# A decoder trunk on one core: a plain first pair for the output projection, and matmuls on constants at the start

## The chip, the cores and the metric

The kernel runs on one core of a Trainium2 chip. Time is device microseconds (us) of one execution. A core has a matrix engine (PE, with its weight loads shown apart as PEld), a vector engine (DVE), a scalar engine (ACT), GpSimd (POOL) and SyncE (SP). Each takes its instructions in the order in which they were written for it. In this kernel SP issues the loads of weights and POOL issues nearly all other transfers. PSUM is the memory that matmuls accumulate in; it is used here in banks.

## The reference

One step of a decoder trunk with two layers, on 520 tokens together (512 of a prompt, 8 of a sample group), width 2048, float32. Per layer:

```
z = rmsnorm(x) @ W_in                      # 2048 -> 8192: conv parts B, C, xc, g and retention parts q, k, v, g
y_conv = B * conv3(C * xc) * silu(g_conv)  # causal, three taps
y_ret  = groupnorm(retention(rope(q), rope(k), v)) * silu(g_ret)    # 4 heads
x = x + concat(y_conv, y_ret) @ W_out      # the output projection
x = x + sigmoid(x @ W_pg) * (p @ W_ple)    # the gate
```

After the second layer comes a last rmsnorm. The states of the convolution and of the retention are outputs too.

## The kernel before

Activations lie transposed: 128 features on the partitions, 520 tokens along a row, in two halves (LEFT and RIGHT) of 260. A projection from 2048 to 2048 has 16 tiles along K (what is summed over) and 16 along M (outputs). M tiles are made two at a time, as **pairs**. A float32 product is three matmuls in a reduced format: each operand is split into a high and a low part by ACT (high) and DVE (low), and high-high, high-low and low-high are added up in PSUM (lines 243, 244, 245). Weights are split in `split_w` (lines 225 and 226) into a ring of 60 tiles whose parts come free when PE has used them; raw weights lie in a ring of 32. Operands are split in `split` (lines 539 and 540).

A pair can be made with Strassen's scheme on its first `s` K tiles and plainly on the rest (`strassen`). It has two M tiles, two halves of the tokens and two halves of these K tiles, so 7 products in place of 8. In matmuls: a plain pair is 16 x 2 x 2 x 3 = 192; Strassen on s tiles takes 3s/2 off. For that DVE adds weights (line 308), and needs sums of operands (`operand_sums`, lines 410 to 413, two new tiles to split for each two K tiles). Partial results are copied from bank to bank and to SBUF while the pair runs, by `copy` (ACT) and `plus` (DVE), which all carry line 296.

How many K tiles each pair takes in Strassen is written in tables: `HEADS`, `CONVS`, `OUT_ROWS` and `GATES`, one list for each layer. `OUT_ROWS` is the output projection's. The class `Operands` builds the operands and their sums for a stage: its list `todo` says for which two K tiles the plain operand, the sums, or both are made, and in which order. Where a table has 0, `pair` makes two single M tiles by `gemm`, one after the other; the first `v` pair of layer 0 is such a one.

There are five PSUM banks for these accumulations (`acc`), handed out in the order in which they came free, and three more for smaller things. `Val` passes a pair's result on, either as SBUF tiles or as the banks themselves.

The order on each engine is not the order of the source. A scheduler places each engine's instructions by a model of time, with a higher priority for weight splits and for `copy` and `plus`. Between engines semaphores keep the dependences, and within an engine the order is fixed: an instruction that waits holds up all behind it.

At the start of the program the first three M tiles are made while inputs arrive, K tile by K tile (lines 655 to 690): SP loads weights and inputs, ACT and DVE split both. Layer by layer there follow the heads' pairs, the convolution's pairs (the last of them with s = 14), the output projection, and the gates.

## Time and profile before

| | |
|---|---|
| time, median of 3 runs | 2204.39 us (2201.32 to 2206.91) |
| the profiled execution: its own time | 2211.48 us |
| its span, first to last instruction | 2209.7 us |
| mean granted PE clock | 0.994 |
| PE busy | 98% of the span, 17854 matmul records |
| DVE, ACT, POOL busy | 86%, 58%, 20% |

The profile's busy shares are averages over stages. "Idle before, releaser" in its rows is the time that an engine stood still ahead of an instruction and the instruction that ended it. PEclk is the clock that PE was granted, 1.00 being all of it. Tile names are without buffer numbers: `ps_g` is any of the five banks, `slot` any of 75 SBUF tiles of 520 columns, `split` and `raw` the rings of weights.

### The profile page before, as it was taken

What the parts mean: (1) busy time and instruction counts of PE and PEld (TensorE: products, weight loads), DVE (VectorE), ACT (ScalarE), POOL (GpSimd) and SP (SyncE); (2) the same over time, 40 slices, a digit from 0 to 9 for tenths busy, and PEclk for the clock granted to TensorE, in tenths of its full rate; (3) what the DMA queues carried; (4) which work ended last, traced back from release to release, by engine and by line L of the source; (5) the groups of instructions that cost most, each with busy time, mean ns of one, the idle gap of its engine ahead of it and who ended that gap; (6) DMA issues with size and microseconds to landing.
All of it is one profiled execution on the core that took longest, in us unless ns stands there. A gap on an engine that the chain in (4) does not pass through costs nothing. (4 is left out here: it accounts for less than half of the span.)

```text
span 2209.7 us, 48509 instructions
## 1 busy us (share of the span) xinstructions
PE 2164.1 (98%) x17854; PEld 2153.7 (97%) x17854; DVE 1906.0 (86%) x3928; ACT 1291.3 (58%) x2789; POOL 443.1 (20%) x764
## 2 busy tenths in 40 slices
PE   8999999999999999999999999999999999999998
PEld 8999999999999899999989999999999999999997
DVE  7789998898999887787997998989998998888874
ACT  8555656555556554565775565655645565555655
POOL 3213222211002210211211222222110031121011
PEclk9999999999999999999999999999999999999999
DMA  7655565555443753745645566664555365556455
GB/s 255 192 170 195 179 222 175 187 160 163 148 144 124 246 172 115 245 150 178 204 143 186 164 205 195 190 214 154 158 172 159 115 197 173 170 187 212 132 161 187
DMA packets 189071, 392.10 MB, mean 177 GB/s; under 512 B 26720, under 2 KB 69728, under 8 KB 188832
## 3 DMA queue, kind: packets, MB, share of 16 engines
q1 hardware_dynamic: 134336, 214.38, 31.2%
q0 software_dynamic: 54496, 174.62, 23.8%
q8 instruction: 140, 2.29, 0.4%
q14 instruction: 99, 0.81, 0.1%
HBM read 323.74 MB, written 65.15 MB: 176 GB/s over the span
## 5 line engine op out<-in xcount | busy, mean ns | idle before, releaser
L243 PE MATMUL ps_g<-slot,split 128*128 128x260 f32 x5496 | 1549.8, 285 | 33.0 <-ACT ps_g L296 13.6
L244 PE MATMUL ps_g<-slot,split 128*128 128x260 f32 x5496 | 1550.8, 284 | 0.0
L245 PE MATMUL ps_g<-slot,split 128*128 128x260 f32 x5496 | 1535.8, 284 | 0.4 <-DVE split L226 0.4
L225 ACT ACTIVATE split<-raw 128x512 fp32r<-128x512 f32 (+2 forms) x1401 | 785.1, 580 | 624.6 <-DVE raw L308 206.7
L243 PEld LDWEIGHTS ps_g<-slot,split 128*128 128x128 f32 x5496 | 1035.6, 189 | 40.5 <-ACT ps_g L296 15.2
L244 PEld LDWEIGHTS ps_g<-slot,split 128*128 128x128 f32 x5496 | 1040.7, 189 | 0.3 <-DVE slot L543 0.3
L245 PEld LDWEIGHTS ps_g<-slot,split 128*128 128x128 f32 x5496 | 1032.6, 189 | 0.9 <-DVE split L226 0.9
L226 DVE TENSOR_TENSOR split<-raw,split 128x512 fp32r<-128x512 f32 (+2 forms) x1401 | 848.1, 627 | 185.4 <-ACT split L225 116.6
L308 DVE TENSOR_TENSOR raw<-raw 128x512 f32<-128x512 f32 (+2 forms) x688 | 427.0, 633 | 24.9 <-DMA raw<-wi 17.8
L296 ACT ACTIVATE slot<-ps_g 128x260 f32<-128x260 f32 x368 | 139.0, 380 | 123.4 <-PE ps_g L245 105.9
L540 DVE TENSOR_TENSOR slot<-slot,slot 128x520 fp32r<-128x520 f32 (+1 forms) x202 | 118.6, 616 | 4.6 <-ACT slot L539 4.0
L539 ACT ACTIVATE slot<-slot 128x520 fp32r<-128x520 f32 (+1 forms) x202 | 104.8, 570 | 11.4 <-DMA slot<-x1s 3.1
L764 POOL DMA_DIRECT2D o_rets<-slot x64 | 35.4, 553 | 344.2 <-DVE slot L763 132.9
L296 DVE TENSOR_TENSOR slot<-ps_g,slot 128x260 f32<-128x260 f32 x184 | 77.3, 421 | 7.6 <-PE ps_g L245 4.6
L1041 POOL DMA_DIRECT2D slot<-x1s x82 | 44.0, 538 | 159.3 <-DVE slot L540 56.2
L852 POOL DMA_DIRECT2D slot<-hs x64 | 46.2, 723 | 119.4 <-PE ps_st L245 31.3
L296 ACT ACTIVATE ps_g<-ps_g 128x260 f32<-128x260 f32 x146 | 54.4, 373 | 20.7 <-PE ps_g L245 20.3
L763 DVE SCALAR_TENSOR_TENSOR slot<-slot,vs,slot 128x256 f32<-128x256 f32 x128 | 55.9, 477 | 8.6 <-ACT slot L759 8.5
L797 POOL DMA_DIRECT2D hs<-slot x64 | 35.6, 557 | 134.5 <-DVE slot L738 66.4
L722 DVE TENSOR_TENSOR slot<-slot,slot 128x520 f32<-128x520 f32 x80 | 55.3, 691 | 7.6 <-DMA o_rets<-slot 7.0
L753 POOL DMA_DIRECT2D slot<-sret x64 | 35.3, 552 | 130.2 <-ACT split L225 36.3
L754 POOL DMA_DIRECT2D slot<-kq x64 | 34.8, 545 | 113.3 <-DVE slot L1090 18.5
(213 smaller groups left out, 1668.5 us busy)
## 6 DMA issues: line engine op xcount, KB each, us to landing
raw<-wi SPq DMA_DIRECT2D x377, 256.0 KB, 4.1
raw<-wi SPq DMA_DIRECT2D x136, 192.0 KB, 4.1
raw<-wo SPq DMA_DIRECT2D x96, 256.0 KB, 4.4
raw<-wg SPq DMA_DIRECT2D x88, 256.0 KB, 4.9
slot<-x1s POOLq DMA_DIRECT2D x82, 260.0 KB, 5.7
hs<-slot POOLq DMA_DIRECT2D x64, 256.0 KB, 3.9
slot<-sret POOLq DMA_DIRECT2D x64, 256.0 KB, 3.9
slot<-hs POOLq DMA_DIRECT2D x64, 256.0 KB, 4.8
```

The costliest lines, as they stand in the source:

```text
L225: S.activation(hi, raw, AF.Copy)
L226: V.tensor_tensor(lo, raw, F(hi), SUB)
L243: PE.matmul(out, wh, xh, start=start, stop=False, skip_group_check=more)
L244: PE.matmul(out, wh, xl, start=False, stop=False, skip_group_check=more)
L245: PE.matmul(out, wl, xh, start=False, stop=stop, skip_group_check=more)
L296: fn(*args)
L308: V.tensor_tensor(out[:, n], x[:, n], y[:, n], op)
L539: keep(S.activation(hi, src[:, n], AF.Copy))
L540: V.tensor_tensor(lo, src[:, n], F(hi), SUB)
L722: V.tensor_tensor(out[:, n], v, table[:, n], MUL)
L763: keep(V.scalar_tensor_tensor(st[:, c], k, vs[:, h, e, b : b + 1], st[:, c], MUL, ADD))
L852: SIDE.dma_start(t[:, :512].rearrange("p (m n) -> p m n", m=2), src)
```

## The change

Four things change; the tables' other lists stay.

1. `OUT_ROWS` goes from [4, 8, 12, 16, 16, 16, 16, 10] to [0, 8, 16, 16, 16, 16, 16, 10] for both layers. Both lists sum to 98, so the output projection has the same number of matmuls.
2. A new function `plain` serves pairs with 0: for each four K tiles it makes both M tiles, into four banks, and returns the banks themselves. It also takes the place of the two `gemm` calls for the first `v` pair of layer 0. `FIRST` keeps the order in which the output projection's operands are made (the first four K tiles with their sums at once), as it was.
3. Eight matmuls of `ones` on `onesd` (128x128, float32, result unused) stand ahead of PE's first work, and the load of `vec` is issued by ACT and not by SP.
4. In the gates the sigmoid is one instruction over 520 columns of an SBUF result, where it was two of 260.

```diff
--- before.py
+++ after.py
@@ -50,7 +50,7 @@
 
 HEADS = [[0, 0, 0, 4, 8, 12] + [14] * 10, [4, 8, 12] + [14] * 13]
 CONVS = [[14] * 2 + [16] * 13 + [14]] * 2
-OUT_ROWS = [[4, 8, 12, 16, 16, 16, 16, 10]] * 2
+OUT_ROWS = [[0, 8, 16, 16, 16, 16, 16, 10]] * 2
 
 MIXED, MIX = 64, [*range(8, 14), *range(8), 14, 15]
 OUTS = [[MIXED + s for s in r] for r in OUT_ROWS]
@@ -58,6 +58,8 @@
 WPRIO = 20
 LATE = 0
 RAW = 32
+WARM = 8
+FIRST = 4
 SPLIT = 60
 
 
@@ -275,6 +277,24 @@
                     product(ps[h], w, j - a, at(x.ops, ks[j : j + 1], n), j == 0, j == KT - 1)
             split_ring.put(*w)
         return Val(banks.put, ps=ps)
+
+    def plain(x, src0, src1):
+
+        ps = acc(4)
+        for a, b in chunks(0, KT):
+            x.supply(min(b + CH, KT))
+            for i, src in enumerate((src0, src1)):
+                w = parts(src, a, b)
+                for j in range(a, b):
+                    for h, n in enumerate((LEFT, RIGHT)):
+                        product(ps[2 * i + h], w, j - a, at(x.ops, [j], n), j == 0, j == KT - 1)
+                split_ring.put(*w)
+            if b == KT // 2:
+                while middle:
+                    middle.pop(0)()
+                aside()
+        aside()
+        return Val(banks.put, ps=ps[:2]), Val(banks.put, ps=ps[2:])
 
     def strassen(x, src0, src1, s, step=None):
 
@@ -390,13 +410,7 @@
         if s:
             z = strassen(x, src[m], src[m + 1], s, (lambda i: x.free(i, nxt)) if last else None)
         else:
-            z0 = gemm(x, src[m], s)
-            while middle:
-                middle.pop(0)()
-            aside()
-            z1 = gemm(x, src[m + 1], s)
-            aside()
-            z = z0, z1
+            z = plain(x, src[m], src[m + 1])
             if last:
                 x.free(8, nxt)
         x.release(n + 1)
@@ -426,7 +440,7 @@
             self.ops = [None] * KT
             self.sums = []
             self.ready = 0
-            first = rows[0] // 2
+            first = max(rows[0], min(FIRST, max(rows))) // 2
             self.todo = [(True, True)] * first + [(True, False)] * (KT // 2 - first)
             self.todo = [(i, *t) for i, t in enumerate(self.todo)]
             self.todo += [(i, False, True) for i in range(first, max(rows) // 2)]
@@ -640,6 +654,11 @@
             return rb
 
 
+    warm = pr.tile([P, 512], F32, tag="r", name="warm")
+    for i in range(WARM):
+        PE.matmul(warm[:, :P], ones, onesd, start=True, stop=True)
+
+
     over = pr.tile([P, 512], F32, tag="r", name="ps_r")[:, :TH]
     first = [acc(2), acc(2), acc(1) + [over]]
     def from_dram(src):
@@ -660,7 +679,7 @@
         if b == 1:
             raw = raw_ring.get(3)
             DMA.dma_start(raw.rearrange("p (m n) -> p m n", n=P), wi[0, 0:3, :, :P].rearrange("m p n -> p m n"))
-            DMA.dma_start(vec, vecs)
+            S.dma_start(vec, vecs)
             x = get()
             for n in (LEFT, RIGHT):
                 DMA.dma_start(x[:, n], xT[0, :, n])
@@ -1167,14 +1186,17 @@
             Gt.need(m // 2 + 1)
             for i, z in enumerate(zs):
                 x = xs[i]
-                for h, (n, ps) in enumerate(zip((LEFT, RIGHT), pes[2 * i : 2 * i + 2])):
-                    v = z.slot[:, n] if z.ps is None else z.ps[h]
-                    S.activation(v, v, AF.Sigmoid)
-                    V.tensor_tensor(v, v, ps, MUL)
-                    V.tensor_tensor(x[:, n], x[:, n], v, ADD)
+                t = get() if z.slot is None else z.slot
+                for n, v in z:
+                    S.activation(t[:, n], v, AF.Sigmoid)
+                if z.slot is None:
+                    z.done()
+                for n, ps in zip((LEFT, RIGHT), pes[2 * i : 2 * i + 2]):
+                    V.tensor_tensor(t[:, n], t[:, n], ps, MUL)
+                    V.tensor_tensor(x[:, n], x[:, n], t[:, n], ADD)
                 if i == 1:
                     banks.put(pes[3])
-                z.done()
+                put(t)
                 if l < DEPTH - 1 or m < SPILL:
                     SIDE.dma_start(x2s[l, m + i], x)
                 rms.add(x)
```

The scheduler makes a new order from it. Rows of the two orders differ at the start, in the output projection and in the gates of both layers.

On ACT, where the last pair of the convolution in layer 0 ends and the output projection begins, before the change (`slot_464` and `slot_465` are the results of that last pair, `ps_g<-ps_g` is the first bank-to-bank copy of the projection's first pair; behind "waits" stand the engines or the DMA queues whose semaphores the instruction waits for):

```order
L225 ACTIVATE split<-raw 128x512 [waits DMAHW6_49,DVE_49,PE_49]
L1047 ACTIVATE slot_524_9849<-gs 128x8 [waits PE_49]
L1047 ACTIVATE slot_523_9846<-gs 128x8 [waits PE_49]
L539 ACTIVATE slot_484_9364<-slot_481_9357 128x260 [waits DVE_49]
L225 ACTIVATE split<-raw 128x512 [waits DMAHW7_49,PE_49]
L225 ACTIVATE split<-raw 128x256 [waits DVE_49]
L225 ACTIVATE split<-raw 128x256 [waits DMAHW0_49]
L225 ACTIVATE split<-raw 128x512 [waits DMAHW5_49,PE_49]
L1047 ACTIVATE slot_536_9961<-gs 128x8
L1047 ACTIVATE slot_535_9958<-gs 128x8 [waits PE_49]
L296 ACTIVATE slot_464_9231<-ps_g 128x260 [waits PE_49]
L296 ACTIVATE slot_465_9232<-ps_g 128x260 [waits DVE_49]
```

and the next row is `L296 ACTIVATE ps_g<-ps_g 128x260 [waits Activation_49]`. With the change the same place reads (lines 225, 296, 539 and 1047 are now 227, 316, 553 and 1066; `slot_463` and `slot_464` are the pair's results):

```order
L316 ACTIVATE slot_464_9240<-ps_g 128x260 [waits PE_49]
L227 ACTIVATE split<-raw 128x512 [waits DMAHW4_49]
L227 ACTIVATE split<-raw 128x512 [waits DMAHW5_49]
L553 ACTIVATE slot_475_9354<-slot_468_9335 128x520 [waits DVE_49]
L553 ACTIVATE slot_479_9362<-slot_477_9358 128x260 [waits DMASW6_49]
L553 ACTIVATE slot_480_9363<-slot_477_9358 128x260
L553 ACTIVATE slot_481_9368<-slot_478_9360 128x520 [waits DMASW7_49]
L1066 ACTIVATE slot_496_9407<-gs 128x8
L1066 ACTIVATE slot_501_9501<-gs 128x8 [waits DVE_49]
L316 ACTIVATE slot_463_9239<-ps_g 128x260 [waits PE_49]
L553 ACTIVATE slot_511_9701<-slot_510_9699 128x260 [waits DMASW6_49]
```

The weight splits that wait for PE no longer stand ahead of the copies that end the pair, and there is no bank-to-bank copy behind them.

On DVE, where the first pair of that projection ends, before the change (`slot_508` and `slot_509` are its results, line 1121 adds them to the residual):

```order
L296 TENSOR_TENSOR slot_509_9577<-ps_g,slot_509_9577 128x260 [waits PE_49]
L226 TENSOR_TENSOR split<-raw,split 128x512 [waits Activation_49] x2
L1121 TENSOR_TENSOR slot_507_9569<-slot_509_9577,slot_507_9569 128x520 [waits Activation_49]
L540 TENSOR_TENSOR slot_520_9839<-slot_517_9832,slot_519_9838 128x520 [waits Activation_49]
L308 TENSOR_TENSOR raw<-raw 128x512 [waits DVE_49]
L296 TENSOR_TENSOR slot_508_9576<-ps_g,slot_508_9576 128x260 [waits PE_49]
L540 TENSOR_TENSOR slot_522_9843<-slot_518_9833,slot_521_9842 128x520 [waits Activation_49]
```

and with it (line 1140 is the addition to the residual, lines 424 to 427 are the operands' sums, 328 the weights' sums; `slot_508` and `slot_509` are now the residual's tiles):

```order
L1140 TENSOR_TENSOR slot_508_9583<-ps_g,slot_508_9583 128x260 [waits PE_49]
L328 TENSOR_TENSOR raw<-raw 128x512 [waits DVE_49]
L554 TENSOR_TENSOR slot_540_9968<-slot_537_9961,slot_539_9967 128x520 [waits Activation_49]
L1140 TENSOR_TENSOR slot_508_9583<-ps_g,slot_508_9583 128x260 [waits PE_49]
L425 TENSOR_TENSOR slot_545_10125<-slot_544_9978,slot_545_10125 128x260 [waits DVE_49]
L1140 TENSOR_TENSOR slot_509_9584<-ps_g,slot_509_9584 128x260 [waits PE_49] x2
L228 TENSOR_TENSOR split<-raw,split 128x512 [waits Activation_49]
```

The residual is added straight from the four banks, so these additions are now what frees them.

On PE, the first rows of the program before the change:

```order
L243 MATMUL ps_g<-slot_3_108,split 128x260 [waits Activation_49]
L243 MATMUL ps_g<-slot_3_108,split 128x260 x2
L243 MATMUL ps_g<-slot_4_109,split 128x260 [waits Activation_49]
L243 MATMUL ps_g<-slot_4_109,split 128x260
L243 MATMUL ps_r<-slot_4_109,split 128x260
```

and with it:

```order
L659 MATMUL warm<-onesd,ones 128x128 [waits Pool_49]
L659 MATMUL warm<-onesd,ones 128x128 x7
L245 MATMUL ps_g<-slot_3_117,split 128x260 [waits Activation_49]
L245 MATMUL ps_g<-slot_3_117,split 128x260 x2
L245 MATMUL ps_g<-slot_4_118,split 128x260 [waits Activation_49]
```

The eight matmuls wait for POOL's constants alone; what follows is as it was.

## The prediction

> **What bounds the kernel now.** I read the page first, then PE's waits, then a table of windows at the places where PE falls behind, then the timelines there. The page:
>
> ```profile
> span 2209.7 us, 48509 instructions
> PE 2164.1 (98%) x17854; PEld 2153.7 (97%) x17854; DVE 1906.0 (86%) x3928; ACT 1291.3 (58%) x2789; POOL 443.1 (20%) x764
> L243 PE MATMUL ps_g<-slot,split 128*128 128x260 f32 x5496 | 1549.8, 285 | 33.0 <-ACT ps_g L296 13.6
> ```
>
> PE is the bound, at 98%. No matmul is taken away (both tables sum to 98), so only time in which PE stands still or runs at half clock can be won. The end of the third row says who ends its stops: ACT's copies from bank to bank. PE's waits split that up:
>
> ```profile
> PE ps_g L243 <- ACT ps_g L296: 13.6, 7, 4.6
> PE ps_g L243 <- ACT slot L296: 8.4, 11, 3.6
> PE ps_g L243 <- ACT slot L542: 6.0, 2, 5.3
> PE ps_g L243 <- DVE slot L296: 2.3, 2, 2.0
> ```
>
> Columns: total us, times, longest. Most of it is the running of Strassen pairs (line 296); 6.0 us is the start. How much of it lies at the two places where the output projection begins, stretches of 15 us show (after each engine: busy us, and instructions):
>
> ```profile
> 700.00:715.00 15.00, 15.00 (x126) 14.85 (x125) 14.24 (x29) 11.34 (x26) 2.67 (x5) 1.00 0.27 85
> 715.00:730.00 15.00, 13.45 (x108) 12.83 (x107) 13.97 (x32) 9.41 (x32) 9.55 (x18) 1.00 0.97 337
> 730.00:745.00 15.00, 12.19 (x75) 11.48 (x75) 13.66 (x32) 9.23 (x33) 2.14 (x4) 0.77 0.84 286
> 745.00:760.00 15.00, 15.00 (x125) 15.00 (x126) 12.76 (x27) 8.78 (x20) 3.22 (x6) 1.00 0.47 149
> 1800.00:1815.00 15.00, 14.20 (x117) 13.99 (x116) 15.00 (x33) 13.59 (x42) 6.38 (x12) 1.00 0.76 241
> 1815.00:1830.00 15.00, 11.55 (x71) 11.04 (x70) 12.73 (x31) 7.89 (x23) 4.79 (x9) 0.77 0.93 337
> 1830.00:1845.00 15.00, 14.84 (x122) 14.43 (x121) 13.26 (x30) 7.19 (x17) 3.76 (x7) 1.00 0.67 216
> ```
>
> Read the count of matmuls: undisturbed it is 125 in 15 us, 0.12 us each. Busy time hides the loss, since a slow matmul is busy too. Layer 0 has 108 + 75 of 250 there, 67 too few, 8.0 us; layer 1 has 117 + 71 + 122 of 375, 65 too few, 7.8 us. That is 15.8 us in all. The column behind POOL's, PEclk, is 0.77 where the count is lowest: the clock was halved for a part of these windows. PE's own timeline in layer 0:
>
> ```profile
> 728.74 0.28 PE L245 MATMUL ps_g<-slot,split 128*128 128x260 f32 x1
> 732.03 0.58 PE L243 MATMUL ps_g<-slot,split 128*128 128x260 f32 x1 [3.02 <-ACT ps_g L296]
> 737.61 0.35 PE L245 MATMUL ps_g<-slot,split 128*128 128x260 f32 x1
> 737.79 0.28 PE L243 MATMUL ps_g<-slot,split 128*128 128x260 f32 x1
> ```
>
> One stop of 3.2 us, and then matmuls of 0.42 instead of 0.28 until 737.6, the slow clock. What ACT did meanwhile:
>
> ```profile
> 728.18 0.63 ACT L225 ACTIVATE split<-raw 128x512 fp32r<-128x512 f32 x1 [4.06 <-PE ps_g L245]
> 729.22 1.75 ACT L225 ACTIVATE split<-raw 128x512 fp32r<-128x512 f32 x4
> 731.07 0.64 ACT L296 ACTIVATE slot<-ps_g 128x260 f32<-128x260 f32 x2
> 731.61 0.38 ACT L296 ACTIVATE ps_g<-ps_g 128x260 f32<-128x260 f32 x1
> ```
>
> ACT stood 4.06 us on a weight split that waits for PE (for a free part of the ring), then did the splits piled up behind it, and only then the last copies of the convolution's pair and the copy of bank a to bank d that the projection's first pair asks for after its first 6 matmuls (s = 4: two K tiles). PE had nothing else in its order. So the stop is one of order: a copy that PE needs at once stands behind splits that PE does not yet need.
>
> **The change part by part.**
>
> *Plain first pair.* It has no bank-to-bank copy, and asks for its banks later: one is free, the others come from the convolution's last pair. In the new order on ACT the two splits ahead of the last copy wait for DMA alone, the copy for the second M tile's bank comes before any split that waits for PE, and PE has 12 matmuls (1.4 us) on the first bank before it asks. So I expect the stop of 3.2 to 3.6 us and the slow clock behind it to go, in both layers. What stays: one wait for a copy into SBUF, at the mean of the second row of waits, 8.4 / 11 = 0.8 us; one at the pair's end, where the four additions on DVE free the banks that the next pair asks for, at the mean of the fourth row, 2.3 / 2 = 1.15; and half a microsecond for an operand that arrives as it is needed (in PE's new order the later K tiles wait for ACT and DVE one by one). That makes 2.5 us of a layer's 7.9, so 5.4 won, **10.8 us** for both. The ends: nothing stays (15.8), or all of it stays and moves (0).
>
> *Pair sizes 8, 16 in place of 8, 12.* Matmuls do not change, 192 + 180 + 168 for 186 + 180 + 174. On DVE the plain pair splits 32 weight tiles, 8 instructions of 512 columns, where the other added and split 11 times 256 columns and split 6 times 512; the third pair gets 24 + 50 to 32 + 56 tiles, 14 more, 3.5 instructions. The sums of operands for 16 K tiles must be ready by the third pair, where it was 12. The rows for it:
>
> ```profile
> L226 DVE TENSOR_TENSOR split<-raw,split 128x512 fp32r<-128x512 f32 x920 | 616.8, 685 | 142.4 <-ACT split L225 80.4 <-PE ps_g L244 46.3 <-PE ps_g L245 4.6
> L226 DVE TENSOR_TENSOR split<-raw,split 128x256 fp32r<-128x256 f32 x129 | 52.3, 417 | 12.2 <-ACT split L225 11.1 <-PE ps_g L245 0.6 <-PE ps_p L244 0.3
> L410 DVE TENSOR_TENSOR slot<-slot 128x260 f32<-128x260 f32 x6 | 2.5, 424 | 0.5 <-DMA slot<-ys 0.4
> 722.00:770.00 48.00, 44.21 (x340) 43.29 (x341) 40.39 (x85) 25.85 (x71) 11.52 (x22) 0.93 0.73 248
> 770.00:790.00 20.00, 20.00 (x169) 20.00 (x169) 17.30 (x35) 10.71 (x25) 2.16 (x4) 1.00 0.50 149
> ```
>
> First pair: 11 x 0.417 + 6 x 0.685 = 8.7 us before, 8 x 0.685 = 5.5 now, 3.2 less. Third pair: 2.4 more. The third row, taken between 716 and 775 us, counts six sums there, and with the two made earlier that is all eight: before the change, too, they are ready when the third pair begins, so they are no new load. From 722 to 770 DVE had 40.4 us of work in 48; without the stop it has some 37 in 42. That fits, with 12% to spare, and I cost it at **nothing**; the cover is DVE's slack, and if it is gone each late sum costs 4 x 0.42 and two splits at 0.69 (the price of 512 columns), 3.1 us. The third pair's window has 17.3 + 2.4 = 19.7 us of DVE in 20.2 of PE (168 matmuls), which has no slack at all if sums slip into it.
>
> *The start.* These rows of SP, ACT and PE carry it, and three windows:
>
> ```profile
> 1.23 0.48 SPq L663 DMA_DIRECT2D vec<-vecs  x1
> 4.78 0.91 ACT L542 ACTIVATE slot<-slot,vec 128x260 fp32r<-128x260 f32 x2 [0.99 <-DMA slot<-xT]
> 5.34 1.45 PE L243 MATMUL ps_g<-slot,split 128*128 128x260 f32 x5 [5.34 <-ACT slot L542]
> 10.25 0.80 PE L243 MATMUL ps_g<-slot,split 128*128 128x260 f32 x2 [0.63 <-ACT slot L542]
> 53.02 1.14 PE L637 MATMUL ps_r<-slot,ones 128*128 128x512 f32 x4
> 54.01 0.37 PE L244 MATMUL ps_g<-slot,split 128*128 128x260 f32 x1
> 5.00:10.00 5.00, 4.27 (x18) 3.97 (x18) 1.45 (x3) 2.28 (x5) 3.42 (x7) 1.00 0.75 241
> 10.00:15.00 5.00, 4.75 (x23) 4.46 (x24) 4.77 (x9) 5.00 (x12) 3.55 (x8) 1.00 1.07 365
> ```
>
> `vec` off SP's queue lets the first input start 0.48 us earlier, and all loads behind it; ACT issues it ahead of its table load, in time that it waits anyway. The first K tile then begins at about 4.9 us. The second, at 10.25, waits for a load among many in flight (DMA share 0.75 to 1.07), so it may gain 0 to 0.5. The matmuls on constants: a float32 one of 512 and one of 8 columns together take 54.01 - 53.02 = 1.0 us at full clock, so one of 128 about 0.25, or 0.5 at half clock, and eight 4.0 us, from about 1.1 (when POOL has written the constants) to 5.1. At worst that is 0.2 us over the first input. From 10.25 to 15 us full clock would fit 39 matmuls; some 23 ran, 16 too few, 1.9 us. In the profile's first windows the clock reads 1.00 though the spacing is that of half; where it says nothing, I go by the spacing.
>
> Does the clock stay up? The first K tile's 18 matmuls end early at full clock, and PE then waits up to 2.5 us for the second. Such a gap is in the trace:
>
> ```profile
> 877.88 0.28 PE L243 MATMUL ps_g<-slot,split 128*128 128x260 f32 x1
> 880.16 0.39 PE L243 MATMUL ps_g<-slot,split 128*128 128x260 f32 x1 [2.00 <-DVE slot L296]
> 881.31 0.42 PE L245 MATMUL ps_g<-slot,split 128*128 128x260 f32 x1
> ```
>
> After 2.2 us of idling the matmuls are slow from 881.1 on. So it can fall back, and the 1.9 us are only partly won. [...] I take **1.5 us** between 0 (clock falls back, second tile no earlier) and 2.4; a loss of 0.2 is the low end.
>
> *The v pair and the sigmoids.* The first v pair changes from two single tiles to both at once: same matmuls, same weights, four banks for two; the next pair then waits for a copy or not, 0.5 us either way, taken as 0. The sigmoids:
>
> ```profile
> L1172 ACT ACTIVATE slot<-slot 128x260 f32<-128x260 f32 x60 | 24.2, 414 | 9.7 <-DVE slot L296 9.2
> L539 ACT ACTIVATE slot<-slot 128x520 fp32r<-128x520 f32 x146 | 86.5, 630 | 7.4 <-DVE slot L411 3.0 <-PE ps_g L245 1.7 <-DVE slot L412 1.4
> ```
>
> 60 x 0.414 become 30 x 0.630, 5.9 us less of ACT, which is 58% busy. It shows only where PE waits on ACT behind them, at the change from gates to the second layer, where three of them stand ahead of a copy; **0.3 us**, between -0.5 (the one sigmoid waits for both halves) and 0.8.
>
> Sum: 10.8 + 0 + 1.5 + 0 + 0.3 = 12.6 us off the profiled execution's 2211.5, to 2199. That execution lies 7.1 us above the median of the runs, which I take as its own; the median goes from 2204.4 to **2192 us**.
>
> **The rivals.**
>
> *The stop moves one pair on.* The second pair (s = 8) begins on the fifth bank and after 12 matmuls, 1.4 us, needs one of the plain pair's four. These come free by additions that have no priority, with a sum of weights (0.68), a split and an operand sum between them on DVE. If they are 2 us late, the clock falls too: 2.0 + 1.7 (3.4 us at half clock) on top of 2.5, so 6.2 of 7.9 stay in each layer. 2 x 1.7 + 1.8 = 5.2 won, **2199 us**. For it: DVE was 91 to 95% busy there (13.66 to 14.24 of 15). Against: DVE has less to do in the new first pair.
>
> *The old stop stays*, because it belongs to the convolution's last pair and the ring, not to Strassen: only the start and the sigmoids count, 1.8 us, **2203 us**. Against: the new order on ACT has other rows there.
>
> *DVE becomes the bound* (slower). Two sums late by the third pair, 6.2 us, the clock after it 1.7, and the 2.4 that its larger s adds: 10.3 us per layer against 5.4 won, 20.6 - 12.6 = 8 us, **2212 us**. It decides from 6.3 us of new waits for DVE per layer on. For it: 19.7 of 20.2 us above. Against: all eight sums were ready in time before.
>
> **How the numbers follow.** The forecast has 0.58, the moved stop 0.26, the old stop 0.07, DVE as the bound 0.09. The forecast's own range is 2187 to 2197; with the moved stop and part of the third the range is **2185 to 2205**, which leaves out most of the slower case and wins beyond the 15.8 + 2.4. What can be told from no change is 0.3%, 6.6 us. Faster by more: the forecast and a quarter of the moved stop, 0.65. Within: the rest of it and the old stop, 0.26. Slower: 0.09.
>
> **What would show it.** In the windows of 15 us around the beginning of the projection, over 115 matmuls in each and PEclk at 1.00, in both layers; PE's waits for ACT's `ps_g` copies down from 13.6 us by 6 to 7; the first 15 us with more than 41 matmuls; the places at 877 to 904 and near 1105 us as they are. I am wrong if DVE's additions to the residual or its operand sums head PE's waits, or if PEclk dips again within 50 us of the projection's start.

## The result, and the profile after

Medians of runs on one chip: before 2205.65 us (2201.32 to 2208.99, 4 runs), changed 2188.61 us (2188.12 to 2190.01, 4 runs). The ratio is 0.9925, 95% interval 0.9906 to 0.9944: 17.0 us, or 0.75%, faster. The forecast was 2192, its range 2185 to 2205.

The page of the changed kernel (own time of this execution 2188.46 us, granted clock 0.997):

```profile
span 2186.6 us, 48458 instructions
PE 2155.9 (99%) x17870; PEld 2148.5 (98%) x17870; DVE 1902.8 (87%) x3910; ACT 1282.4 (59%) x2735; POOL 441.8 (20%) x764
L245 PE MATMUL ps_g<-slot,split 128*128 128x260 f32 x5500 | 1543.0, 284 | 18.5 <-ACT ps_g L316 8.1
```

The idle time ahead of that line's matmuls went from 33.0 to 18.5 us. PE's waits (total, times, longest):

```profile
PE ps_g L245 <- ACT ps_g L316: 8.1, 4, 4.2
PE ps_g L245 <- ACT slot L316: 7.5, 7, 1.3
PE ps_r L631 <- DVE slot L1284: 1.7, 1, 1.7
PE ps_g L245 <- ACT slot L556: 1.4, 1, 1.4
```

Bank-to-bank copies ended 13.6 us of stops and end 8.1 now. The wait for the first operands (ACT's `slot` split, 6.0 before) is 1.4. No addition to the residual is among them. The table of windows, first of before, then of the changed kernel, shows the two places where the projection begins and the three others where a stage begins:

```profile
700.00:760.00 60.00, 55.64 (x431) 54.16 (x430) 54.62 (x117) 38.76 (x108) 17.57 (x33) 0.94 0.64 214
1800.00:1860.00 60.00, 55.59 (x431) 54.46 (x430) 51.59 (x110) 36.99 (x98) 17.62 (x33) 0.94 0.73 239
870.00:930.00 60.00, 53.47 (x417) 52.84 (x416) 45.76 (x102) 31.59 (x76) 16.59 (x31) 0.94 0.71 238
```

```profile
5.00:10.00 5.00, 3.41 (x20) 2.69 (x20) 1.95 (x4) 2.90 (x6) 3.21 (x7) 1.00 0.87 282
10.00:15.00 5.00, 4.75 (x39) 4.76 (x40) 5.00 (x11) 5.00 (x12) 3.71 (x10) 1.00 1.05 367
700.00:760.00 60.00, 59.39 (x495) 59.18 (x494) 56.83 (x120) 39.37 (x107) 19.25 (x36) 1.00 0.73 255
720.00:735.00 15.00, 15.00 (x127) 15.00 (x127) 15.00 (x32) 12.49 (x44) 5.12 (x10) 1.00 1.04 391
1800.00:1860.00 60.00, 58.50 (x482) 57.79 (x481) 54.41 (x106) 33.76 (x77) 14.88 (x28) 1.00 0.69 233
870.00:930.00 60.00, 55.49 (x446) 54.87 (x445) 51.20 (x113) 38.23 (x86) 16.60 (x31) 0.97 0.70 237
1075.00:1120.00 45.00, 39.74 (x314) 38.85 (x313) 38.99 (x89) 40.06 (x85) 12.49 (x21) 0.96 0.68 235
1950.00:2010.00 60.00, 56.55 (x468) 55.93 (x467) 51.62 (x105) 38.43 (x80) 17.65 (x33) 1.00 0.69 242
```

Count the matmuls: undisturbed, 837 run in 100 us, so 502 fit in 60 us. The projection's beginning was short by 71 in each layer, and is now short by 7 and 20, so 115 are regained, 13.7 us at 0.119 us each. DVE is full from 720 to 735 us (15.00 of 15) and PE is full beside it. What ACT does there (its timeline in the changed kernel):

```profile
712.57 0.37 ACT L316 ACTIVATE slot<-ps_g 128x260 f32<-128x260 f32 x1
712.84 0.41 ACT L227 ACTIVATE split<-raw 128x256 fp32r<-128x256 f32 x1
717.20 0.63 ACT L227 ACTIVATE split<-raw 128x512 fp32r<-128x512 f32 x1 [3.95 <-DMA raw<-wo]
...
721.18 0.36 ACT L316 ACTIVATE slot<-ps_g 128x260 f32<-128x260 f32 x1
```

ACT still stands 4 us on a weight split, now for its load, and PE runs on: 127 matmuls from 705 to 720 us. The stop on ACT is no longer PE's.

Where the time went along the program is read from the start of each matmul: both kernels issue the same number, so the n-th of one trace is set against the n-th of the other (those on constants left out). Below, rounded, is how much earlier (minus) each stage was passed than in the profiled execution of before, in us, stage by stage. "rest" is all behind the second projection.

```
                first 500  heads,conv 0  projection 0  gates 0  heads,conv 1  projection 1  rest    sum
changed           -1.3       -1.7          -7.7        -4.5       0.0          -6.4         -1.5   -23.0
rows alone         0.2       -1.8          -6.1        -3.1       0.5          -6.7         -3.4   -20.3
single tiles       0.0       -1.9          -8.2        -5.2       0.4          -7.7         -1.6   -24.1
sizes 8, 12       -1.7       -0.5          -7.6        -4.2       4.5          -7.8         -1.8   -19.1
sums early        -0.2       -1.1          -7.7        -5.0       0.9          -6.9          0.2   -19.9
all beginnings    -0.5       -2.5          -7.6        -4.3      -3.6          -8.8         -4.1   -31.4
start alone       -0.9       -0.9           1.1        -6.2       0.9           1.2         -2.9    -7.7
8, 8, 8           -0.2       -2.5           6.6        -6.4       0.2           3.3         -1.6    -0.5
ring 62           -0.9       -2.5           0.9        -2.8       0.1           2.5         -2.2    -4.9
ring 64            1.0       -1.7          -0.4        -5.6      -0.5          -2.6         -5.1   -14.8
no sums of weights 0.0       -2.0           1.5        -4.7       0.3          -1.6         -2.5    -8.9
no bank copies     0.1       -1.6           2.4        -5.0      -1.5          -1.2         -1.5    -8.1
neither           -0.2       -2.4          -4.6        -3.4      -1.1          -1.2         -1.9   -14.8
```

The other rows are the experiments below; each is one profiled execution. The columns "heads, conv 0", "gates 0" and "rest" are negative for nearly every kernel, those that keep the old projection too: the profiled execution of before was slow there. It lay 5.8 us above the median of before, and had a stop of 3.6 us near 903 us that "start alone", which has nothing else new at that place, does not show either. So of the 23.0 us between the two profiles, 14.1 are the two projections, 1.3 the start, and most of the 7.6 left is that one execution; between the medians it is 17.0.

### The profile page after: what moved, and what is told of

It is laid out like the page before. It is cut to its first block, busy times and chain, and to the rows that moved or that the text cites. A ratio compares the mean times of both kernels' runs of the same rounds, so it can differ in the third digit from the quotient of the medians.

```text
span 2186.6 us, 48458 instructions
## 1 busy us (share of the span) xinstructions
PE 2155.9 (99%) x17870; PEld 2148.5 (98%) x17870; DVE 1902.8 (87%) x3910; ACT 1282.4 (59%) x2735; POOL 441.8 (20%) x764
## 4 chain that ended last, share of the span: by engine, by line
PE 86%; DMA 5%; issue 3%; ACT 3%; DVE 3%; POOL 1%; SPq 0%; DVEq 0%; ACTq 0%; POOLq 0%
PE ps_g L245 27%; PE ps_g L247 27%; PE ps_g L246 27%; DMA raw<-wg 1%; ACT split L227 1%; DVE split L228 1%; DMA o_rets<-slot 1%; DMA slot<-x2s 1%; DMA slot<-xT 1%; ACT slot L553 1%; DMA raw<-wi 0%; DVE raw L328 0%; POOL slot L1060 0%; DMA raw<-wo 0%; ACT slot L476 0%
## 5 line engine op out<-in xcount | busy, mean ns | idle before, releaser
L245 PE MATMUL ps_g<-slot,split 128*128 128x260 f32 x5500 | 1543.0, 284 | 18.5 <-ACT ps_g L316 8.1
```

Of the source, the lines that this page charges most:

```text
L245: PE.matmul(out, wh, xh, start=start, stop=False, skip_group_check=more)
```

## The experiments

Each run is set against before on its own chip: a median of 2209.01 us for rows alone, single tiles and the two rings; 2204.83 for start alone, sizes, 8, 8, 8 and all beginnings; 2207.93 for sums early and the three kernels that leave something out. Times between these groups are compared by ratio.

**Which part wins.** *The rows alone*: the changed kernel without the matmuls on constants, with `vec` on SP and the two sigmoids of 260 columns (the `v` pair stays side by side).

```diff
-    for i in range(WARM):
-        PE.matmul(warm[:, :P], ones, onesd, start=True, stop=True)
...
-            S.dma_start(vec, vecs)
+            DMA.dma_start(vec, vecs)
...
-                t = get() if z.slot is None else z.slot
-                for n, v in z:
-                    S.activation(t[:, n], v, AF.Sigmoid)
+                for h, (n, ps) in enumerate(zip((LEFT, RIGHT), pes[2 * i : 2 * i + 2])):
+                    v = z.slot[:, n] if z.ps is None else z.ps[h]
+                    S.activation(v, v, AF.Sigmoid)
...
```

> The plain first pair and its table alone: the start (no matmuls on constants, vec loaded by SP) and the two sigmoids of 260 columns are as before the change. In 60 us around the projection's start (700 to 760, 1800 to 1860) the kernel before has 431 matmuls in each layer, the changed one 495 and 482, of 500 that fit. Theory (the gain is the projection's start): 490 or more and 475 or more here too, and a time 13 to 16 us under the kernel before (ratio 0.993 to 0.994). Rival (the three parts share the gain, or the start shifts everything that follows): under 470 in one of the layers, or less than 10 us.

Measured: 2191.69 us, ratio 0.9922 (0.9896 to 0.9948); 482 and 483 matmuls in the windows 700 to 760 and 1800 to 1860. Within the noise all of the gain is there without the start and the sigmoids.

*The start alone*, put into the kernel before.

```diff
...
+    for i in range(WARM):
+        PE.matmul(warm[:, :P], ones, onesd, start=True, stop=True)
...
-            DMA.dma_start(vec, vecs)
+            S.dma_start(vec, vecs)
```

> The kernel before with the start alone: the eight matmuls on constants, and the load of vec issued by ACT. Theory 1 (the start is worth what it wins there and keeps it): the 500th matmul 1.2 to 2 us earlier than before, the windows 700 to 760 and 1800 to 1860 as before (431 within 10), the time 1 to 3 us lower. Theory 2 (what the start wins is lost again at the next stop, where ACT or DVE is the one that is late): the 500th matmul is earlier but the last one within 0.5 us of before.

Measured: 2201.21 us, ratio 0.9986 (0.9974 to 0.9997), 422 and 417 matmuls. The 500th matmul is 0.9 us earlier, a little under the 1.2 that theory 1 wanted; the time falls by 3.1 us with an interval from 0.7 to 5.7, so the start does win a little. The projection wins nothing (1.1 and 1.2 us later in the table). Six kernels with the new start pass the 500th matmul 0.8 us early on the mean (+0.0 to -1.7), seven with the old one at 0.0 (+1.0 to -0.9).

*Single tiles*: the projection's first pair made as two M tiles one after the other (two banks each), not side by side. The `v` pair stays side by side.

```diff
-            z = plain(x, src[m], src[m + 1])
+            if nxt is None:
+                z = plain(x, src[m], src[m + 1])
+            else:
+                z0 = gemm(x, src[m], s)
...
+                z1 = gemm(x, src[m + 1], s)
...
+                z = z0, z1
```

> The changed kernel, with the projection's first pair as two single M tiles one after the other in place of side by side (the v pair stays side by side). Theory 1 (no copy between banks is all that matters): as the changed kernel, within 2 us. Theory 2 (side by side matters too): the first M tile uses up a K tile in 6 matmuls, 0.72 us, in place of 12, so all 16 in 11.5 us; the last K tile, made of the convolution's last pair, was split some 14 us after that pair's end before the change, so PE stops 2 to 5 us in each layer for operands, with 1.7 us of slow clock where it is over 2 us: 4 to 13 us slower than the changed kernel.

Measured: 2187.52 us, ratio 0.9908 (0.9888 to 0.9927); 500 and 492 matmuls. What wins is that the pair is plain. Side by side adds nothing that shows here.

*The sizes* 8, 12, ..., 14 in place of 8, 16, ..., 10 behind the plain pair.

```diff
-OUT_ROWS = [[0, 8, 16, 16, 16, 16, 16, 10]] * 2
+OUT_ROWS = [[0, 8, 12, 16, 16, 16, 16, 14]] * 2
```

> The changed kernel with OUT_ROWS [0, 8, 12, 16, 16, 16, 16, 14] for both layers (sum 98): the third pair stays at 12 as before the change, and the last takes the four. Theory 1 (the sizes behind the plain pair do not matter, DVE has the slack): within 3 us of the changed kernel, the windows 700 to 760 and 1800 to 1860 over 480 matmuls. Theory 2 (the sums for 16 K tiles come late in the third pair): 3 to 8 us faster than the changed kernel. Theory 3 (a larger last pair, 14 for 10, frees operands and banks for the gates later): 2 to 6 us slower, lost between 850 and 930 us.

Measured: 2193.35 us, ratio 0.9955 (0.994 to 0.9971); 495 and 492 matmuls. In the projection the sizes do nothing (-7.6 and -7.8 us in the table, -7.7 and -6.4 with 16). Yet the whole is 0.3% worse than the changed kernel by the two ratios (their intervals overlap a little, so this is not clear of the noise), and no theory had the place: in this one execution 4.5 us are lost in the second layer's heads and convolution. A window there, of this kernel, has 104 matmuls where the changed kernel has 127:

```profile
1140.00:1155.00 15.00, 13.02 (x104) 12.41 (x102) 15.00 (x31) 7.42 (x17) 2.50 (x5) 1.00 0.36 107
```

The edit changes nothing of that stage but the scheduler's order, which is written anew from the projection on. That the order is the cause is argued, not shown.

**Why a Strassen pair stops PE there.** The prediction said: order on ACT; a copy that PE needs at once stands behind weight splits that wait for a free part of the ring. If so, a larger ring alone should win. *Ring of 62*, then *ring of 64*, in the kernel before:

```diff
-SPLIT = 60
+SPLIT = 62
```

> The kernel before with 62 in place of 60 tiles in the ring of split weights; Strassen with s = 4 stays. It moves the order on ACT: in layer 0 the first copy from bank to bank now stands ahead of all splits that wait for PE; in layer 1 three such splits still stand between the convolution's last copies and that copy. Theory (the stop is a copy behind splits that wait for the ring): layer 0 loses at most 3 us in the 60 us around the projection's start (475 matmuls or more), layer 1 5 to 9 us (425 to 460). Rival (Strassen on 4 K tiles stops PE by itself, whatever the order): 425 to 450 in both layers.

> The same with 64 tiles. Here the order on ACT is the other way round: in layer 0 three splits that wait for PE stand ahead of the first copy from bank to bank, in layer 1 that copy stands ahead of them. Theory: layer 0 loses 5 to 9 us (425 to 460 matmuls in the 60 us), layer 1 at most 3 (475 or more). Rival: 425 to 450 in both.

Measured, one execution each: 2207.15 us with 423 and 414 matmuls, and 2197.23 us with 435 and 449. So the order theory fails for layer 0 of the first (423 for 475 or more), and is at best half right for the second (435 as it wanted, 449 for 475 or more). PE's stops from 705 to 750 us with a ring of 62, and then of 64, have other names:

```profile
PE ps_g L244 <- DVE slot L540: 2.1, 2, 1.0
PE ps_g L243 <- ACT slot L539: 1.8, 1, 1.8
```

```profile
PE ps_g L243 <- ACT slot L296: 2.1, 1, 2.1
PE ps_g L243 <- ACT split L225: 2.0, 2, 1.1
PE ps_g L243 <- ACT ps_g L296: 1.0, 2, 0.5
```

In place of one stop of 3.0 us there are several of 0.5 to 2 us, for operands, weight splits and copies in turn. The order on ACT is not out of it. With 64 tiles ACT stood 4.4 us on a weight split in layer 0, for its load, and the copy for which PE stopped 2.1 us stood behind it:

```profile
720.55 0.42 ACT L225 ACTIVATE split<-raw 128x256 fp32r<-128x256 f32 x1 [4.43 <-DMA raw<-wo]
```

With 62 tiles it stood 3.3 us on one in layer 1, for PE, ahead of the bank copy for which PE then stopped 2.8 us. What all of these kernels share is the Strassen pair on four K tiles, with products of 6 matmuls, 0.7 us. *8, 8, 8*: the same sum of 98, still Strassen first, but with products of 12 matmuls.

```diff
-OUT_ROWS = [[4, 8, 12, 16, 16, 16, 16, 10]] * 2
+OUT_ROWS = [[8, 8, 8, 16, 16, 16, 16, 10]] * 2
```

> The kernel before with OUT_ROWS [8, 8, 8, 16, 16, 16, 16, 10] for both layers (the same sum of 98): the projection's first pair is still Strassen, with all its copies and sums of weights, but on 8 K tiles, so that PE has 12 matmuls (1.4 us) and not 6 (0.7 us) between one product and the next. Theory 1 (a Strassen pair on few K tiles stops PE, because a product of 0.7 us is shorter than the chain of copy, sum of weights and split that the next one needs while ACT and DVE are loaded): the windows 700 to 760 and 1800 to 1860 us, 431 matmuls each before, get over 470, and the time falls by 8 to 14 us. Theory 2 (any Strassen pair at that place stops PE; only a plain one helps): 425 to 450 matmuls, and a time within 5 us of before.

Measured: 2212.25 us, ratio 1.0037 (1.0025 to 1.005), slower; 376 and 403 matmuls. PE's waits from 1795 to 1865 us, and a row of ACT's timeline there:

```profile
PE ps_g L243 <- ACT split L225: 6.2, 2, 5.5
```

```profile
1820.91 0.63 ACT L225 ACTIVATE split<-raw 128x512 fp32r<-128x512 f32 x1 [2.30 <-DMA raw<-wo]
```

Longer products do not help, and the counts lie below what either theory named: now PE waits 5.5 us for one weight split, and ACT ahead of it 2.3 us for a load. That left two theories: what a Strassen pair itself asks for (sums of weights, copies), or the load of DVE at that place. *Sums early* puts work of DVE earlier there, in the changed kernel, by building the sums of the first eight K tiles at once and not of the first four.

```diff
-            first = max(rows[0], min(FIRST, max(rows))) // 2
+            first = max(rows[0], min(8 if rows[1] == 8 else FIRST, max(rows))) // 2
```

> The changed kernel, with the first eight and not the first four K tiles of the output projection's operands built together with their sums. Nothing is added, the work of two more pairs of sums (8 x 0.42 us for sums and 4 x 0.69 for splits on DVE, 6.1 us, and four splits of 0.63 on ACT) is only done earlier, at the projection's beginning, where DVE is busy 14 to 15 of 15 us. Theory L (it is the load of DVE and ACT at the beginning of the projection that makes PE stop, whatever the pair): the windows 700 to 760 and 1800 to 1860 us, 495 and 482 matmuls in the changed kernel, fall below 470, the time rises by 4 to 12 us. Theory C (it is the copies or the sums of weights of a Strassen pair, which the plain one lacks): both stay over 480, the time within 2 us of the changed kernel.

Measured: 2190.70 us, ratio 0.9913 (0.9892 to 0.9933); 494 and 487 matmuls, DVE 15.00 of 15 from 720 to 735:

```profile
720.00:735.00 15.00, 15.00 (x125) 14.78 (x124) 15.00 (x34) 12.22 (x42) 5.85 (x11) 1.00 0.99 345
```

In this window the edit adds nothing, since DVE was full there without it (15.00, 127 matmuls). In layer 1 it does: from 1800 to 1830 us DVE goes from 26.6 to 29.6 us of 30, and the matmuls from 240 to 241. So here, where the pair is plain, PE ran on beside a full DVE: 125 matmuls in these 15 us with the edit, 127 without. Theory L falls in this form. *No sums of weights*, *no bank copies*, and *neither*, each in the first pair of the projection of the kernel before (the third has both edits; the sums left out are four in the code, not three as the expectation says):

```diff
         def add(out, x, y, op):
+            if cut:
+                return
...
```

> The kernel before, with the three sums of weights left out in the projection's first pair (the products use the raw weights, so the two M tiles are not what they should be); its copies stay. Theory A (the chain of load, sum on DVE, split on ACT, split on DVE is what comes late): the windows 700 to 760 and 1800 to 1860, 431 matmuls each before, rise over 470, the time falls by 8 us or more. Theories C and L: at most 450 in each.

```diff
-        copy(d, a)
+        if not cut:
+            copy(d, a)
...
-        copy(z1[:, RIGHT] if c is None else c, b)
+        if not cut:
+            copy(z1[:, RIGHT] if c is None else c, b)
...
```

> The kernel before, with the two copies from bank to bank left out in the projection's first pair (those banks begin with a new sum, so the two M tiles lack one product each); sums of weights and copies into SBUF stay. Theory C (PE waits for the copy of a bank that it must go on adding to): both windows over 470, the time 8 us or more below before. Theories A and L: at most 450 in each.

> The kernel before with both left out in the projection's first pair, sums of weights and copies from bank to bank; what stays of Strassen is the order of the products, the sums of operands and the copies into SBUF. If the copies and the sums of weights together are the cause: both windows over 470, and 10 us or more below before, also where either alone does little. Theory L: at most 450, since the operands' sums and the convolution's last work on DVE stay where they are.

Measured:

```
                     time us   ratio (95%)               700 to 760   1800 to 1860
no sums of weights   2199.33   0.9967 (0.9952 to 0.9982)    420           442
no bank copies       2206.61   0.9992 (0.9979 to 1.0005)    417           437
neither              2195.36   0.9936 (0.9918 to 0.9954)    472           443
```

By the windows neither theory A nor theory C holds alone. In layer 0 PE waits 5.0 us for a bank copy when the sums are away, and 3.5 us for a copy into SBUF when the bank copies are; in layer 1 it then waits 2.8 us for a weight split. With both away, layer 0 gets 472 matmuls, and the time is 2195.36 us; over 470 in both layers was expected, and layer 1 does not get there. By the times the sums count for more: without them the time falls by 7.3 us (4.0 to 10.6; theory A wanted 8 or more), without the bank copies by 1.8 (-1.1 to 4.6), without both by 14.1. The windows are of one execution each, and that of no sums of weights, 2203.23 us, lay 3.9 above its median. ACT's timeline without bank copies:

```profile
727.89 0.63 ACT L225 ACTIVATE split<-raw 128x512 fp32r<-128x512 f32 x1 [3.88 <-DMA raw<-wo]
...
731.49 0.64 ACT L299 ACTIVATE slot<-ps_g 128x260 f32<-128x260 f32 x2
```

It is the picture of before: a split that waits 3.9 us, splits piled up behind it, and then the copies that end the convolution's pair, for which PE waits now (3.5 us) instead of for the bank copy. Here the split waits for its load and not for the ring.

In layer 1 "neither" has 443. The three windows of 15 us there show why:

```profile
1800.00:1815.00 15.00, 14.67 (x122) 14.46 (x121) 14.08 (x33) 9.77 (x31) 4.80 (x9) 1.00 1.02 377
1815.00:1830.00 15.00, 15.00 (x127) 15.00 (x126) 12.18 (x26) 8.36 (x17) 2.69 (x5) 1.00 0.59 208
1830.00:1845.00 15.00, 10.84 (x73) 10.24 (x72) 12.02 (x24) 7.14 (x17) 4.31 (x8) 0.89 0.72 214
```

Up to 1830 us it runs like the changed kernel; then it loses 54 of 127 matmuls, 6.4 us, one pair later, with the sums and copies of that pair in place:

```profile
1833.01 0.36 PE L243 MATMUL ps_g<-slot,split 128*128 128x260 f32 x1 [1.39 <-DVE slot L299]
1838.33 0.39 PE L243 MATMUL ps_g<-slot,split 128*128 128x260 f32 x1 [2.31 <-ACT split L225]
```

This is the first rival of the prediction, the stop that moves to the second pair, though in another kernel. The changed kernel does not have it.

What is shown: the six kernels with a plain first pair have 482 to 501 matmuls in the two windows, and the seven with a Strassen pair, two of them with its sums or its bank copies left out, have 376 to 449; "neither" stands between, with 472 and 443. It is not one lucky order: in layer 1 ACT's order differs from kernel to kernel (in layer 0 five of the six plain ones have nearly the same). What stays open: whether one thing within the Strassen pair is the worst. Each kernel that leaves something out also has a new order, and the two were not told apart. A plain pair also leaves its results in the banks, where "neither" still copies them to SBUF; what that is worth by itself was not measured. Loads of the weights are one suspect: in several of these kernels ACT stands for them, and the DMA's share is 0.9 to 1.04 from 720 to 735 us. But ACT stands 3.95 us for such a load in the changed kernel too, where it costs PE nothing. The ring of raw weights and the order of loads were not varied.

**The same edit elsewhere.** Three other stages begin with Strassen on four K tiles, and the changed kernel is short there by 56 (870 to 930), 63 (1075 to 1120) and 34 (1950 to 2010), at 502 in 60 us. (The expectation below counted in windows of 15 us, in which matmuls on a border count twice, and has smaller numbers.)

```diff
-HEADS = [[0, 0, 0, 4, 8, 12] + [14] * 10, [4, 8, 12] + [14] * 13]
+HEADS = [[0, 0, 0, 4, 8, 12] + [14] * 10, [0, 8, 16] + [14] * 13]
...
-GATES = [[4, 8, 12, 16, 16, 16, 16, 10], [4, 8, 12] + [14] * 4 + [0]]
+GATES = [[0, 8, 16, 16, 16, 16, 16, 10], [0, 8, 16] + [14] * 4 + [0]]
```

> The changed kernel with the same two edits at the other three places where a stage begins with a Strassen pair on four K tiles: GATES [0, 8, 16, ...] for [4, 8, 12, ...] in both layers, and HEADS [0, 8, 16, ...] for [4, 8, 12, ...] in the second. The sums of the tables are kept, so the matmuls are the same in number. In the changed kernel these places are short by 47 matmuls of 500 (870 to 930 us), 58 of 375 (1075 to 1120 us) and 24 of 500 (1950 to 2010 us), 15.5 us together. Theory 1 (a small Strassen pair at the start of a stage is what stops PE, whatever the stage): four fifths of it is won, as in the projection, 10 to 13 us, some 2176 us. Theory 2 (the projection was special, since its results are added straight from the banks; in the gates a bank comes free only by a sigmoid on ACT, and in the heads by work of rope or convolution): under 4 us won, 2185 to 2195 us, with waits for ACT's sigmoid or its copies at the same places.

Measured: 2180.63 us, ratio 0.9898 (0.988 to 0.9916), the fastest of all. By the two ratios that is 0.27% or 6 us better than the changed kernel, with intervals that just overlap; between the two profiled executions it is 8.4 us. Hoped for were 10 to 13. Its windows at the three places:

```profile
870.00:930.00 60.00, 54.89 (x443) 54.48 (x442) 47.69 (x101) 34.98 (x74) 18.14 (x34) 0.97 0.74 253
1075.00:1120.00 45.00, 44.98 (x370) 44.29 (x369) 40.29 (x89) 39.18 (x80) 12.28 (x20) 1.00 0.68 245
1950.00:2010.00 60.00, 59.65 (x495) 59.20 (x494) 49.02 (x94) 34.27 (x67) 14.44 (x27) 1.00 0.75 270
```

The second layer's heads (370 for 314) and gates (495 for 468) run almost freely, as theory 1 has it. The first layer's gates do not (443 for 446): PE now stops 3.85 us in the last pair of the projection, where ACT stands on weights that are not loaded yet ahead of the copy that PE needs (ACT's timeline).

```profile
882.62 0.94 ACT L227 ACTIVATE split<-raw 128x384 fp32r<-128x384 f32 x2 [2.22 <-DMA raw<-wo]
883.47 0.37 ACT L316 ACTIVATE slot<-ps_g 128x260 f32<-128x260 f32 x1
```

And some of what the heads' beginning won is given back in the same stage (3.6 us gained over the stage, where the 56 matmuls at its beginning are 6.7 us).

## Why the prediction was right, and where it was not

*The plain first pair*: right in its place and sign, too small. It forecast 10.8 us for both layers and measured 13.7 by the counts, 14.1 by the starts of the matmuls, near its upper end of 15.8. The step that was mis-sized is "what stays", 2.5 us per layer: 7 and 20 matmuls, 0.8 and 2.4 us, stayed. Of its three parts the copy into SBUF came in layer 1 alone (1.2 us); the 0.6 us of layer 0, at 750.6 us, are a bank copy of the second pair. The 1.15 us for the residual's additions came in neither: no such wait is in the trace.

*The reason given for it*, "the stop is one of order: a copy that PE needs at once stands behind splits that PE does not yet need", is half of the cause. It was read in layer 0, and the claim that PE's own splits hold up the ring does not carry over to layer 1: there the split on which ACT stood, in the kernel before, waited for its load.

```profile
1819.64 0.63 ACT L225 ACTIVATE split<-raw 128x512 fp32r<-128x512 f32 x1 [2.43 <-DMA raw<-wo]
```

In layer 0 before, start alone, no sums of weights, no bank copies and the ring of 64 each show ACT standing 3.9 to 4.4 us on a split, for the ring or for a load, ahead of copies for which PE then stops. But with the ring of 62 it does not stand so there (2.0 us at most), and layer 0 still has 423 matmuls: several short stops take the place of the long one. And in the changed kernel ACT stands 3.95 us without a stop of PE. What decides is that a Strassen pair at that point makes PE wait for ACT and DVE again and again; a plain one needs neither copies nor sums of weights. That copies and sums do it together is argued: taking both away wins 14.1 us, the sums alone 7.3, the bank copies alone nothing clear of noise, and the windows follow in part only (472 in layer 0 and 443 in layer 1 without both). That a late weight split or a late operand can hold PE up as a late copy does (5.5 us for a split in 8, 8, 8, 1.8 us for an operand with the ring of 62) was not in the prediction.

*The sizes at nothing*: right for the projection. The cover was named as DVE's slack, and there was less of it than worked out: DVE is busy 39.8 of 42 us from 722 to 764, where some 37 was forecast, and from 720 to 735 it has none (15.00 us of 15); PE ran 127 matmuls there all the same. The window that the prediction took for the third pair, 770 to 790 us, lies half in the second, whose results are added to the residual at 781 and 785 us. In the changed kernel the third pair runs from about 769 to 789 us, with 16.1 us of DVE work in 20, not 19.7 in 20.2. Outside the projection the sizes may matter, by 0.3%, through a stage that the prediction did not look at.

*The start*: 1.5 us forecast, 1.3 in this trace, 0.8 as the mean of six kernels. The matmuls on constants took 3.78 us for the 4.0 worked out, and the clock is up from 5.9 us on (14.1 before):

```profile
1.14 3.78 PE L659 MATMUL warm<-onesd,ones 128*128 128x128 f32 x16 [1.14 <-POOL half_neg L598]
...
7.72 0.28 PE L247 MATMUL ps_r<-slot,split 128*128 128x260 f32 x1
9.45 0.51 PE L245 MATMUL ps_g<-slot,split 128*128 128x260 f32 x2 [1.44 <-ACT slot L556]
```

The gap ahead of the second K tile, feared at 2.5 us, is 1.4, and the clock stays up through it (1.00 from 10 to 15 us, with 39 matmuls). The start's upper end, 2.4 us, was the author's estimate, the 1.9 us of the clock and the 0.5 us of the second tile won whole; no run shows it, the most at the 500th matmul was 1.7 us. That the clock stayed up was luck in part: in two of the six kernels with the new start (sums early, all beginnings) the clock fell back, as the prediction feared, in sums early after a gap of 2.2 us (0.66 from 10 to 15 us, below). And the kernel before was a late one. With the old start the clock is first up at 8.6 to 15.0 us in eight kernels, and with the new one at 4.0 to 6.0 in six; yet in the first 15 us the eight have 37 to 59 matmuls and the six 41 to 61. So the 59 for 41 of these two traces, one of the signs that the prediction named, shows little by itself. Sums early, with the new start, and no bank copies, with the old one:

```profile
10.00:15.00 5.00, 4.65 (x23) 4.44 (x24) 4.96 (x10) 5.00 (x12) 4.00 (x9) 0.66 1.05 355
```

```profile
10.00:15.00 5.00, 5.00 (x41) 4.75 (x40) 5.00 (x11) 5.00 (x11) 3.83 (x10) 1.00 1.07 365
```

*The v pair and the sigmoids*: the heads' column in the table is -1.6 us on the mean of the six kernels with the new v pair, and -1.9 on that of the seven with the old, so nothing. The sigmoids' 0.3 us is below what these runs can tell; it was not measured by itself.

*The base*: taking the profiled execution of before as slow, and the median as its own, was right (7.1 us above the median of three runs, 5.8 above that of four), and the table now shows in which stages it was slow. *"The places at 877 to 904 and near 1105 us as they are"*: the second is; the first shows 446 for 417, which is that execution and not the change: the seven other kernels that keep the projection's Strassen pair have 430 to 459.

*The rivals*: the stop did not move to the second pair, the old one did not stay, and DVE became full but not the bound. The 3.4 us at half clock that two of them count are as long as the slow stretch from 881.1 to 884.5 us in the kernel before, at 0.51; there a stop of 2.0 us went ahead of it, and in single tiles none followed one of 2.75 us. Two signs were missed by little: PE's waits for bank copies fell by 5.5 us where 6 to 7 were named, and one window of layer 1, 1800 to 1815 us, has 114 matmuls where over 115 were. The sum of 12.6 was short of 17.0 by the 3.3 us of the plain pair; the last microsecond is within what the medians can tell.

## What to carry to other kernels

Where a stage begins, the engines that feed PE still have the last stage's work queued; a scheme that saves matmuls there at the price of copies and sums in PE's path can cost more than it saves: here the 6 matmuls saved are 0.7 us, and the beginning was short by 71, 8.4 us, in each layer. Put the saving where operands are ready, and begin with the plain form: the same edit at two more stages won matmuls again. Before naming one late instruction as the cause, take it away: twice here the wait only changed its name. And an engine at 100% in a window is no proof that it binds (DVE at 15.00 of 15 us, with PE's 127 matmuls beside it); the counts of PE beside it are.

## What the hardware showed unexpectedly

In these traces the length of one stop of PE does not by itself tell whether its clock falls. In the single-tiles kernel PE stood 2.75 us and went on at full clock. The same execution, after ten matmuls of one column and only 0.89 us of standing, fell to half clock at 45.4 us. In the kernel before, 2.0 us were enough, as the prediction quotes.

```profile
42.55 1.17 PE L640 MATMUL ps_r<-ones,slot 128*128 128x1 f32 x10
44.83 0.39 PE L245 MATMUL ps_g<-slot,split 128*128 128x260 f32 x1 [0.89 <-ACT slot L755]
...
889.83 0.39 PE L245 MATMUL ps_g<-slot,split 128*128 128x260 f32 x1 [2.75 <-ACT slot L316]
```

Here are two windows of 3.41 us in the kernel before, at its stop of 2.0 us, and then four in single tiles, at its two stops:

```profile
877.73:881.14 3.41, 1.41 (x12) 1.21 (x11) 3.34 (x9) 1.53 (x4) 0.00 (x0) 0.99 0.00 0
881.14:884.56 3.42, 3.42 (x19) 3.42 (x18) 3.42 (x10) 2.41 (x8) 0.54 (x1) 0.51 0.00 0
```

```profile
41.95:45.36 3.41, 2.52 (x22) 2.33 (x21) 3.41 (x11) 3.41 (x8) 0.12 (x1) 1.00 0.47 154
45.36:48.77 3.41, 3.41 (x18) 3.41 (x18) 2.30 (x7) 3.41 (x10) 3.03 (x1) 0.50 0.20 62
885.10:888.51 3.41, 1.98 (x17) 1.77 (x15) 1.14 (x3) 0.02 (x1) 0.02 (x1) 1.00 1.03 385
888.51:891.92 3.41, 2.09 (x17) 2.09 (x18) 2.38 (x7) 2.76 (x8) 1.08 (x2) 1.00 0.88 329
```

In the kernel before PE is busy 1.41 of the 3.41 us around its stop, and the next window reads 0.51. In single tiles the window with the ten matmuls of one column shows 2.52 us of work, and the next reads 0.50; the two windows that share the stop of 2.75 us show 1.98 and 2.09 us of work, and both read 1.00. So neither the length of a stop nor PE's busy time in such a window puts these three cases in order. What lowers the clock was not shown.
